# Where three kinds of small transfers are issued in a woven encoder step: head results, carried rows and cached keys

## The chip, the core and the metric

The kernel runs on one core of one Trainium2 chip. A time is the device time of one execution in microseconds (us), and the kernel's time is the median of several runs. The profile is of one execution; its trace lists every instruction with its start and length, and for idle time of an engine what ended it.

The engines are TensorE (PE: matmuls and transposes, its weight loads apart as PEld), VectorE (DVE), ScalarE (ACT), GpSimd (POOL) and SyncE (SP), which here does nothing but issue transfers. Each engine takes its instructions in program order.

## The reference

One step of an encoder layer for two groups of rows that share all weights: a prompt of 2048 rows and 8 samples of 16 rows (128 in all), width 1024, everything in 32-bit floats.

```
h     = RMSNorm(x) * (1 + scale1) + shift1
cols  = h @ w_in                      # columns belong to four mixers A, B, C, D with 4 heads each
A: gated delta rule    B: stick-breaking attention
C: softmax attention with a forget bias    D: softmax attention over 9 chunks of 64 rows, with a relative bias
mixed = [A | rms_norm(B) * merge_g[0] | rms_norm(C) * merge_g[1] | rms_norm(D) * merge_g[2]]   # per head
x     = x + gate1 * (mixed @ w_o)
h     = RMSNorm(x) * (1 + scale2) + shift2
a, b  = causal_conv3(h @ w_up)        # the samples start from state_ffn_conv, 2 rows for each
x     = x + gate2 * ((silu(a) * b) @ w_down)
```

A head has 64 columns, so `merge_g` is a row of 64 numbers for each head of B, C and D. The samples attend to cached keys and values too: 1024 rows for each sample in B and C, 512 in D.

## The kernel before

**The work and its stages.** Two kinds of streams are woven into one program. The dense stream first makes the projection in four parts of 512 rows, then four feed-forward blocks of 512 rows (the last also takes the 128 sample rows, and is called block 3 here). The mixer stream runs the delta rule and the attention of B, C and D for one part after another; such a stretch, one letter and one part, is called a pool here, since it has a tile pool of its own. There are 12 of them, with 4 heads each, so 48 heads. The samples' attention for B, C and D runs beside the parts. While a mixer waits for a chain through DVE, ACT and POOL, TensorE is to work on dense matmuls. The order of the instructions on each engine is set by `weave` and `merge`, which take turns between the streams, and then by the tile scheduler, which goes by a simulated timeline with priorities. So an edit that changes when something is due can move rows of the program far from it.

**Transfers.** Nearly all are issued from SP in program order, only some start-up loads from POOL. Eight semaphores (DMAHW0 to DMAHW7) are used in turn, so a transfer of SP waits until the one eight before it has landed. An instruction of SP that waits also holds all that is queued behind it.

**A head.** `head(h)` loads the head's queries `qT`, the forget bias (C) or the relative bias (D) as `add`; `start_k` and `start_v` load its keys `kT` and values `vhl`. `front` makes the scores (on TensorE `z<-kT,qT`) and weights, `back` the products with the values (`oT`). At the end of a head's last unit, `head_norm` (from L863) does this:

```
mg = A.sp.tile([P, 64], F32, name="hg", bufs=1)
nc.sync.dma_start(out=mg, in_=K.I["merge_g"][0, gi, h:h + 1].to_broadcast([P, 64]))
sq = A.sp.tile([P, nt, 64], F32, name="nsq", bufs=1)
...
nc.gpsimd.tensor_tensor(sq, sq, mg.unsqueeze(1).to_broadcast([P, nt, 64]), op=ALU.mult)
nc.sync.dma_start(out=dst, in_=sq)
```

POOL squares (L869), DVE sums (L871), a reciprocal root of several Newton steps follows between DVE and POOL (L203 to L217), DVE scales (L873), POOL multiplies by the gain (L874), and SP stores 128 KB to `mixed` (L875). `nsq` has one buffer, so the next head's squaring also waits until the store has landed. On POOL there also run the products of pool B's weights (L743), clears of parts of the tiles `wh` and `wl` (L834, L835) and the copies of feed-forward rows (L1890, L1915).

**Cached keys of the samples.** `keys` (from L1542) loads 512 rows of a sample's cached keys as one tile `ck` of 512 KB with one buffer (L1533), turns them with 8 transposes on TensorE (`ptr<-ident,ck`), and copies the result to `ckT` in two copies, taken in turn by DVE (L71) and ACT (L73). There are 40 such loads. The projected q and k of the new rows come first, in tiles of the same names (L1502).

**Feed-forward block 3.** Its start loads the weights `w_o` (in tiles `wu`, L1801), then `mixed` (in tiles `raw`, L1690), which TensorE turns (`d<-ident,raw`) before the product with `w_o`. For each chunk of 128 of the 5632 up-projected columns, in 44 calls of `up(fi)`, the carried rows of `state_ffn_conv` are loaded as a tile `stn` of 16 x 128 (8 KB, L1896, two buffers) and turned on TensorE (`ptr<-ident,stn`). The tiles `wd` (L1937) hold weights of the down-projection.

Of the kernel before, what the change touches and what calls it, by code (L numbers as in the profile page):

```python
# [5 lines left out]
F32 = mybir.dt.float32  # L6
# [9 lines left out]
P = 128  # L16
# [843 lines left out]
                nc.vector.tensor_scalar(oh[:, i - base, :], po[:, y * 64:y * 64 + 64], rls[i - 2 * jj], None, op0=ALU.mult)  # L860


def head_norm(K, A, gi, h, oh, nt, dst):  # L863

    nc = K.nc
    mg = A.sp.tile([P, 64], F32, name="hg", bufs=1)
    nc.sync.dma_start(out=mg, in_=K.I["merge_g"][0, gi, h:h + 1].to_broadcast([P, 64]))
    sq = A.sp.tile([P, nt, 64], F32, name="nsq", bufs=1)
    nc.gpsimd.tensor_tensor(sq, oh, oh, op=ALU.mult)  # L869
    ss = K.small.tile([P, nt], F32, name="nss")  # L870
    nc.vector.tensor_reduce(ss, sq, axis=AX.X, op=ALU.add)  # L871
    r = rsqrt(K, K.small, ss, nt, 1.0 / 64, EPS, "rsn")
    nc.vector.tensor_tensor(sq, oh, r.unsqueeze(2).to_broadcast([P, nt, 64]), op=ALU.mult)  # L873
    nc.gpsimd.tensor_tensor(sq, sq, mg.unsqueeze(1).to_broadcast([P, nt, 64]), op=ALU.mult)  # L874
    nc.sync.dma_start(out=dst, in_=sq)  # L875


def attn_prompt(K, g, part):


    nc = K.nc
    gi = "BCD".index(g)
# [3 lines left out]
    A = Ctx()  # L886
# [12 lines left out]
    def head(h):  # L899
        H = Ctx()  # L900
        H.h, H.kT, H.v = h, {}, {}
        H.qT = A.sp.tile([P, 2, 512], F32R, name="qT", bufs=2)
        nc.sync.dma_start(out=f(H.qT), in_=rows(K.qT[g][part], h))
        H.oh = A.sp.tile([P, 4, 64], F32, name="oh", bufs=2)
        if g == "C":
            fb = A.sp.tile([P, s1 * 512], F32, name="add", bufs=1)
            nc.sync.dma_start(out=fb.rearrange("p (t c) -> p t c", c=P),
                              in_=K.nF[0:16 * s1].rearrange("(t h) p -> h t p", h=4)[h:h + 1].to_broadcast([P, 4 * s1, P]))
            H.add = lambda a, b, c1: fb[:, a:b]
        if g == "D":  # L910
            bias = A.sp.tile([P, 640], F32, name="add", bufs=2)
            nc.sync.dma_start(out=bias, in_=K.toep(h))
            nc.gpsimd.memset(bias[0:64, 576:640], NEG)
            nc.gpsimd.memset(bias[64:128, 0:64], NEG)
            H.add = lambda a, b, c1: bias[:, a + 640 - c1:b + 640 - c1]
        return H
# [43 lines left out]
    def back(u):  # L960
        H, jj = u.H, u.jj
        if u.first:
            u.st.V = Values(K, A, jj, lo, u.st.wts, H.v, *((2 * jj, 0) if g == "B" else (lo(2 * jj), 2 * jj)))
        for a in u.groups:
            u.st.V.group(a)
            yield
        if u.last:
            u.st.V.finish(None if g == "B" else [w.rl for w in u.st.wts], H.oh, 4 * part)
            if jj == j0 + 1:
                yield  # L970
                r, c = 4 * part * P, (1 + gi) * 256 + H.h * 64
                head_norm(K, A, gi, H.h, H.oh, 4, K.mixed[r:r + 512, c:c + 64].rearrange("(t p) d -> p t d", p=P))

    units = []
    for h in range(4):
        hs = Ctx()
        hs.h = h
        for jj in (j0, j0 + 1):
            st = Ctx()
            for s in range(jj // 2, -1, -1) if g == "B" else [None]:  # L980
                u = Ctx()
# [26 lines left out]
    with K.tc.tile_pool(name=f"a{g}{part}", bufs=2, side="right", reuse_waits="tile") as A.sp:  # L1008
        yield from start_k(units[0])
        for n, u in enumerate(units):  # L1010
            u.H = u.hs.H
            parts = [(front(u), u.nf)]
            if n:
                b = units[n - 1]
# [474 lines left out]
def samples_steps(K, A, g):  # L1489
    nc, I, sp, psum = K.nc, K.I, A.sp, A.psum  # L1490
    gi = "BCD".index(g)
    name = {"B": "sb", "C": "fox", "D": "band"}[g]
    ck, cv = I[f"cache_{name}_k"], I[f"cache_{name}_v"]
# [4 lines left out]
        segs = segs[::-1]  # L1498
    x0 = []
    for n, src in (("k", K.qs[g]), ("v", K.ks[g])):  # L1500
        t = sp.tile([P, 4 if n == "k" else 2, 256], F32, name="c" + n, bufs=1 if n == "k" else 2)[:, 0]
        nc.sync.dma_start(out=t, in_=src)  # L1502
        x0.append(t)
    qn, kn = x0
# [8 lines left out]
    if g == "D":  # L1513
        bias = sp.tile([P, 640], F32, name="sbias", bufs=1)
        for h in range(8):
            r = slice(h * 16, h * 16 + 16)
# [3 lines left out]
    pt = psum()  # L1520
# [3 lines left out]
    for o in range(2):  # L1524
        r = slice(o * 64, o * 64 + 64)
# [3 lines left out]

    def load(b, s):  # L1530

        t = sp.tile([P, 4, 256], F32, name="ck", bufs=1)
        nc.sync.dma_start(out=t, in_=ck[0, b, s * 512:(s + 1) * 512].rearrange("(t p) h d -> p t (h d)", p=P))  # L1533
        return t

    def load_v(b, kt):

# [4 lines left out]
    def keys(L, b, s):  # L1542

        L.kT[s] = []
        for u in range(2):
            k = load(b + u, s)
            kT = sp.tile([P, 2, 512], F32, name="ckT", bufs=2)
            L.kT[s].append(kT)
            for x in range(2):
                pt = psum()  # L1550
                for j in range(4):
                    K.pe.transpose(pt[:, j * P:(j + 1) * P], k[:, j, x * P:x * P + P], K.ident)
                A.ev.copy(kT[:, x], pt)
                yield

    def weights(L, b):
# [80 lines left out]
NF = 22  # L1637
# [133 lines left out]
def feed_block(K, B, sa, sp, nxt, pool, copies):  # L1771


    nc, I, O = K.nc, K.I, K.O
    T, tiles, GM, ahead, acc, p = B.T, B.tiles, B.GM, B.ahead, B.acc, B.p
    smp = NP in tiles
# [62 lines left out]
    n = len(tiles)  # L1839
    pt = K.dps()  # L1840
# [32 lines left out]
    def carry():  # L1873
# [8 lines left out]
            nc.sync.dma_start(out=O["ffn_conv_s"][:, cc], in_=eo[2:18])  # L1882
        late.clear()

    def up(fi):

        cw = K.fcw[:, fi]
# [4 lines left out]
        if smp:  # L1892
            us = u[:, 2 + Tp:2 + Tp + NB * 18].rearrange("p (b s) -> p b s", s=18)
            parts.append((lambda i: us[:, :, i:i + 16], s16(yv[:, Tp:T])))
            stn = sp.tile([16, P], F32, name="stn", bufs=2)
            nc.sync.dma_start(out=stn, in_=I["state_ffn_conv"][0, :, :, fi * P:(fi + 1) * P].rearrange("b r c -> (b r) c"))  # L1896

        def evict(ps, c0, c1):
            m = min(c1, Tp)
# [262 lines left out]
```

## Time and profile before

| | |
|---|---|
| median of 3 runs | 3899.07 us (3897.04 to 3899.76) |
| the profiled execution's own time | 3892.44 us |
| its span in the trace | 3890.7 us |
| mean granted TensorE clock | 0.967 |
| TensorE busy | 3628.3 us, 93% of the span |
| VectorE, ScalarE, GpSimd busy | 2437.3, 1537.0, 1406.7 us |
| moved by transfers | 830.36 MB, 213 GB/s in the mean |

The span lies 1.7 us below the execution's own time. The profiled execution is 6.6 us faster than the median of the runs.

In the rows of the trace that follow, a row of the timeline has the start, the length, the engine and line, the operation, the tile written and the tiles read, how many rows were merged, and in brackets how long the engine had been idle and what ended that. `SPq` is the issue of a transfer on SP: its length is that of the issuing, not of the transfer. A row of the list of waits says who waited, for whom, and then the total in us, how often, and the longest. A group of one line has the shortest, median and longest duration in ns.

### The profile page before, as it was taken

To read this page: it belongs to the slowest core of one execution; us is meant where nothing else is said; L and a number is where in the kernel's file an instruction comes from. 1 tells how busy PE (TensorE), PEld (TensorE's weight loads), DVE (VectorE), ACT (ScalarE), POOL (GpSimd) and SP (SyncE) were. 2 spreads that over 40 slices of the span, in tenths; PEclk is the share of its full clock that TensorE was granted. 3 is DMA by queue.
4 is the path that set the end of the run, shared out by engine and by line. 5 is a ranking of instruction groups with operands and counts; after the bars stand their busy time and mean duration, and the time that the engine had idled before them with its cause. 6 is when DMAs were issued, how large, how long until landed. Compare 5 with 4: busy or idle time off the path is not lost.

```text
span 3890.7 us, 66224 instructions
## 1 busy us (share of the span) xinstructions
PE 3628.3 (93%) x22763; PEld 3147.3 (81%) x22763; DVE 2437.3 (63%) x5592; ACT 1537.0 (40%) x3352; POOL 1406.7 (36%) x3487
## 2 busy tenths in 40 slices
PE   6998899989988999999999999989999987899999
PEld 4887889989986667767877888668887876899999
DVE  5668556465676876877595656755875665344344
ACT  3455223343454533543463533413553443232221
POOL 4456244363333444434571112323652122122121
PEclk7999999999998999999999999999999998899999
DMA  7887868877668798987536555665445545444442
GB/s 225 290 279 245 300 199 299 295 256 246 218 227 255 254 307 274 306 293 270 200 120 213 171 201 169 226 209 178 158 148 182 177 123 206 141 149 137 153 143 93
DMA packets 529077, 830.36 MB, mean 213 GB/s; under 512 B 112651, under 2 KB 351260, under 8 KB 528477
## 3 DMA queue, kind: packets, MB, share of 16 engines
q1 hardware_dynamic: 527269, 825.16, 64.2%
q8 instruction: 181, 2.97, 0.3%
q0 software_dynamic: 1472, 0.97, 0.1%
q14 instruction: 155, 1.26, 0.1%
HBM read 611.81 MB, written 224.16 MB: 215 GB/s over the span
## 4 chain that ended last, share of the span: by engine, by line
PE 62%; DMA 11%; DVE 9%; POOL 4%; issue 3%; ACT 2%; SPq 1%; POOLq 0%; DVEq 0%; ACTq 0%
PE d L89 44%; PE z L89 5%; PE oT L89 5%; PE ptr L92 4%; PE ptr L89 2%; PE d L92 1%; DVE pr L741 1%; DMA w<-win 1%; DMA add<-nF 1%; DVE gy L1184 1%; DVE cv L1913 1%; DMA wraw<-in_ada_w_dram 1%; DMA raw<-in_x_prompt_dram 1%; PE z L92 1%; DVE acc L1823 1%
## 5 line engine op out<-in xcount | busy, mean ns | idle before, releaser
L89 PE MATMUL d<-hh,wu 128*128 128x512 f32 (+1 forms) x3520 | 1013.9, 364 | 2.8 <-DMA wu<-keptw_up 1.6
L89 PEld LDWEIGHTS d<-hh,wu 128*128 128x128 f32 x3520 | 635.2, 190 | 94.6 <-issue 8.6
L89 PE MATMUL d<-w,hh 128*128 128x256 f32 (+2 forms) x3536 | 679.3, 288 | 30.3 <-DMA w<-win 9.7
L89 PE MATMUL d<-hl,wu 128*128 128x512 f32 (+1 forms) x1760 | 638.8, 363 | 0.8 <-DVE hl L1863 0.7
L89 PEld LDWEIGHTS d<-w,hh 128*128 128x128 f32 x3536 | 557.6, 191 | 48.6 <-DVE w L459 11.8
L89 PE MATMUL d<-gh,wd 128*128 128x512 f32 (+1 forms) x1760 | 529.8, 369 | 10.3 <-DVE acc L1823 8.1
L89 PE MATMUL d<-w,hl 128*128 128x256 f32 (+2 forms) x1768 | 502.3, 286 | 0.2 <-DVE hl L408 0.2
L1913 DVE SCALAR_TENSOR_TENSOR cv<-u,fcw,cv 128x512 f32<-128x512 f32 (+1 forms) x440 | 300.1, 705 | 174.2 <-ACT cv L1911 170.9
L1823 DVE SCALAR_TENSOR_TENSOR acc<-d,mod,acc 128x512 f32<-128x512 f32 (+2 forms) x432 | 280.8, 656 | 188.4 <-PE d L89 187.1
L89 PEld LDWEIGHTS d<-hl,wu 128*128 128x128 f32 x1760 | 334.0, 190 | 43.9 <-DVE hl L1863 3.0
L89 PEld LDWEIGHTS d<-gh,wd 128*128 128x128 f32 x1760 | 319.1, 189 | 60.3 <-DVE acc L1823 13.6
L89 PEld LDWEIGHTS d<-w,hl 128*128 128x128 f32 x1768 | 336.3, 191 | 4.8 <-issue 3.3
L89 PE MATMUL d<-gl,wd 128*128 128x512 f32 (+1 forms) x880 | 319.4, 363 | 0.0
L89 PE MATMUL z<-kT,qT 128*128 128x512 f32 (+3 forms) x864 | 255.8, 385 | 34.7 <-DMA kT<-kTD 13.8
L840 ACT CAST wh<-ptr 128x512 fp32r<-128x512 f32 (+1 forms) x372 | 197.4, 552 | 226.8 <-PE ptr L92 133.6
L841 DVE TENSOR_TENSOR wl<-ptr,wh 128x512 fp32r<-128x512 f32 (+1 forms) x372 | 232.3, 639 | 79.5 <-ACT wh L840 69.1
L1900 ACT COPY u<-d 128x512 f32<-128x512 f32 (+1 forms) x220 | 109.9, 500 | 396.5 <-PE d L89 391.0
L92 PE MATMUL ptr<-ident,w 128*128 128x128 f32 x1448 | 225.1, 277 | 18.9 <-POOL w L743 8.2
L741 DVE TENSOR_TENSOR_SCAN pr<-sn,pr,zeros 128x512 f32<-128x512 f32 (+3 forms) x172 | 217.8, 1275 | 24.3 <-ACT sn L733 18.8
L1915 POOL COPY hal<-u 128x2 f32<-128x2 f32 x176 | 44.5, 254 | 519.7 <-ACT u L1900 516.2
L743 POOL TENSOR_TENSOR w<-w,pr 128x512 f32<-128x512 f32 (+3 forms) x168 | 190.8, 1138 | 112.1 <-DVE pr L741 60.2
L790 ACT ACTIVATE w<-w,nm 128x512 f32<-128x512 f32 (+3 forms) x284 | 174.1, 615 | 120.5 <-DVE nm L783 98.1
(610 smaller groups left out, 7116.5 us busy)
## 6 DMA issues: line engine op xcount, KB each, us to landing
wu<-keptw_up SPq DMA_DIRECT2D x264, 512.0 KB
w<-win SPq DMA_DIRECT2D x132, 512.0 KB
wd<-keptw_down SPq DMA_DIRECT2D x132, 512.0 KB
keptw_up<-wu SPq DMA_DIRECT2D x88, 512.0 KB
wu<-keptw_o SPq DMA_DIRECT2D x48, 512.0 KB
win<-w SPq DMA_DIRECT2D x44, 512.0 KB
raw<-in_w_up_dram SPq DMA_DIRECT2D x88, 256.0 KB
keptw_down<-wd SPq DMA_DIRECT2D x44, 512.0 KB
```

The costliest lines, as they stand in the source:

```text
L89: return self.note(self.nc.tensor.matmul(out, lhsT, rhs, **k))
L92: return self.note(self.nc.tensor.transpose(*a, **k))
L741: nc.vector.tensor_tensor_scan(out=pr[:, 0:m][:, ::-1], data0=sn[:, :m][:, ::-1], data1=K.zeros[:r, :m], initial=carry, op0=ALU.mult, op1= ...
L743: nc.gpsimd.tensor_tensor(w[:, :m], w[:, :m], pr[:, 1:m + 1], op=ALU.mult)
L790: self.K.nc.scalar.activation(w, w, AF.Exp, bias=self.nm, accum_out=self.l[:, s:s + 1])
L840: nc.scalar.copy(wh[:, c0:c1], pt[:, c0:c1])
L841: nc.vector.tensor_tensor(wl[:, c0:c1], pt[:, c0:c1], f(wh[:, c0:c1]), op=ALU.subtract)
L1184: nc.vector.scalar_tensor_tensor(yc, tap(c, i), self.cw[:, c, i:i + 1], yc, op0=ALU.mult, op1=ALU.add)
L1823: nc.vector.scalar_tensor_tensor(acc[k][:, c0:m], ps[:, :m - c0], gate[:, k, 0:1], acc[k][:, c0:m], op0=ALU.mult, op1=ALU.add)
L1900: nc.scalar.copy(u[:, 2 + c0:2 + m], ps[:, :m - c0])
L1913: nc.vector.scalar_tensor_tensor(o, tap(i), cw[:, i:i + 1], o, op0=ALU.mult, op1=ALU.add)
L1915: nc.gpsimd.tensor_copy(K.hal[:, fi], tail)
```

## The change

It has three parts.

- In the attention over the prompt, the gain tile `hg` is loaded in `head()` together with the head's queries, with two buffers, no longer in `head_norm`. The store to `mixed` is issued by POOL, right behind the multiply, no longer by SP. `nsq` keeps its one buffer.
- A tile `ck` of the samples holds 256 rows (256 KB) in place of 512, with two buffers. There are twice as many loads, with as many transposes and copies as before; a copy now takes both column halves of two row blocks and writes them to two places of `ckT`.
- The carried rows `stn` of block 3 are loaded three chunks ahead: three loads at the start of the block, then one in each `up`, into four buffers in place of two.

```
-def head_norm(K, A, gi, h, oh, nt, dst):
+def head_norm(K, A, mg, oh, nt, dst):
...
-    mg = A.sp.tile([P, 64], F32, name="hg", bufs=1)
-    nc.sync.dma_start(out=mg, in_=K.I["merge_g"][0, gi, h:h + 1].to_broadcast([P, 64]))
     sq = A.sp.tile([P, nt, 64], F32, name="nsq", bufs=1)
...
-    nc.sync.dma_start(out=dst, in_=sq)
+    nc.gpsimd.dma_start(out=dst, in_=sq)
...
         H.oh = A.sp.tile([P, 4, 64], F32, name="oh", bufs=2)
+        H.mg = A.sp.tile([P, 64], F32, name="hg", bufs=2)
+        nc.sync.dma_start(out=H.mg, in_=K.I["merge_g"][0, gi, h:h + 1].to_broadcast([P, 64]))
...
-        t = sp.tile([P, 4 if n == "k" else 2, 256], F32, name="c" + n, bufs=1 if n == "k" else 2)[:, 0]
+        t = sp.tile([P, 2, 256], F32, name="c" + n, bufs=2)[:, 0]
...
     def load(b, s):
 
-        t = sp.tile([P, 4, 256], F32, name="ck", bufs=1)
-        nc.sync.dma_start(out=t, in_=ck[0, b, s * 512:(s + 1) * 512].rearrange("(t p) h d -> p t (h d)", p=P))
-        return t
+        ts = [sp.tile([P, 2, 256], F32, name="ck", bufs=2) for _ in range(2)]
+        for n, t in enumerate(ts):
+            c = s * 512 + n * 256
+            nc.sync.dma_start(out=t, in_=ck[0, b, c:c + 256].rearrange("(t p) h d -> p t (h d)", p=P))
+        return ts
...
-            k = load(b + u, s)
             kT = sp.tile([P, 2, 512], F32, name="ckT", bufs=2)
             L.kT[s].append(kT)
-            for x in range(2):
+            for n, k in enumerate(load(b + u, s)):
                 pt = psum()
-                for j in range(4):
-                    K.pe.transpose(pt[:, j * P:(j + 1) * P], k[:, j, x * P:x * P + P], K.ident)
-                A.ev.copy(kT[:, x], pt)
+                for x in range(2):
+                    for j in range(2):
+                        c = (2 * x + j) * P
+                        K.pe.transpose(pt[:, c:c + P], k[:, j, x * P:x * P + P], K.ident)
+                A.ev.copy(kT[:, :, n * 256:n * 256 + 256], pt.rearrange("p (x n) -> p x n", x=2))
                 yield
...
+    state, ahead_of = [], [c for j in range(NF) for c in (j, NF + j)] if smp else []
+
+    def state_load():
+
+        if ahead_of:
+            fi = ahead_of.pop(0)
+            state.append(sp.tile([16, P], F32, name="stn", bufs=4))
+            nc.sync.dma_start(out=state[-1], in_=I["state_ffn_conv"][0, :, :, fi * P:(fi + 1) * P].rearrange("b r c -> (b r) c"))
+
+    for _ in range(3):
+        state_load()
...
-            stn = sp.tile([16, P], F32, name="stn", bufs=2)
-            nc.sync.dma_start(out=stn, in_=I["state_ffn_conv"][0, :, :, fi * P:(fi + 1) * P].rearrange("b r c -> (b r) c"))
+            stn = state.pop(0)
+            state_load()
```

SP has 2661 transfers before and 2653 now (48 stores fewer, 40 key loads more). Below stand SP's rows at three places, each with what the row waits for: DMAHW is the landing of an earlier transfer of SP, DMASW of one of POOL, and Pool, PE, DVE and Activation are engines.

The first place is the end of pool C and the start of pool D, both of part 3, before:

```order
L1801 DMA wu_38524<-keptw_up_89 128x1024 [waits DMAHW3_49,PE_49]
L875 DMA mixed_80<-nsq_38004 128x4x64 [waits DMAHW0_49,Pool_49]
L903 DMA qT_38033<-qTD_116 128x1024 [waits DMAHW1_49,DVE_49]
L912 DMA add_38036<-skew_3924 128x640
L998 DMA kT_38040<-kTD_114 128x512 [waits PE_49,Activation_49]
L998 DMA kT_38042<-kTD_114 128x512 [waits DMAHW4_49]
```

The same place now (line numbers are a few higher in the changed kernel):

```order
L1805 DMA wu_38606<-keptw_up_89 128x1024 [waits DMAHW4_49,DMAHW0_49,PE_49]
L902 DMA qT_38113<-qTD_116 128x1024 [waits DVE_49]
L905 DMA hg_38116<-in_merge_g_dram 128x64
L913 DMA add_38118<-skew_3924 128x640
L999 DMA kT_38122<-kTD_114 128x512 [waits PE_49,Activation_49]
L999 DMA kT_38124<-kTD_114 128x512 [waits DMAHW1_49]
```

The store of pool C's last head, which waits for POOL, stood ahead of pool D's first loads; it is on POOL's queue now, and pool D's first hg takes a place there that waits for no engine.

The second place is inside that pool D, where its first two heads end, before (`out_0` are stores of block 2's results):

```order
L875 DMA mixed_80<-nsq_38425 128x4x64 [waits Pool_49]
L867 DMA hg_38765<-in_merge_g_dram 128x64 [waits DMAHW6_49]
L1735 DMA out_0_dram<-raw_38736 128x512 [waits DMAHW7_49,Activation_49]
L1735 DMA out_0_dram<-raw_38744 128x512 [waits DMAHW0_49,DVE_49]
L1735 DMA out_0_dram<-raw_38801 128x512 [waits DMAHW1_49,Activation_49]
L1735 DMA out_0_dram<-raw_38809 128x512 [waits DMAHW2_49,DVE_49]
L1005 DMA vhl_39092<-vhlD_115 128x512 [waits DMAHW3_49,PE_49]
L875 DMA mixed_80<-nsq_38767 128x4x64 [waits DMAHW4_49,Pool_49]
L867 DMA hg_39063<-in_merge_g_dram 128x64 [waits DMAHW6_49,DMAHW5_49]
```

The same place now:

```order
L905 DMA hg_38678<-in_merge_g_dram 128x64 [waits Pool_49]
L1739 DMA out_0_dram<-raw_38820 128x512 [waits DMAHW3_49,Activation_49]
L1739 DMA out_0_dram<-raw_38828 128x512 [waits DMAHW4_49,DVE_49]
L1739 DMA out_0_dram<-raw_38883 128x512 [waits DMAHW5_49,Activation_49]
L1739 DMA out_0_dram<-raw_38891 128x512 [waits DMAHW6_49,DVE_49]
L1006 DMA vhl_39174<-vhlD_115 128x512 [waits DMAHW7_49,PE_49]
L905 DMA hg_39033<-in_merge_g_dram 128x64 [waits DMAHW0_49,Pool_49]
```

The stores of heads 0 and 1 are gone from here, and the gains of heads 2 and 3 stand in their places; each waits for POOL, because the buffer that it takes is free only when the multiply of the head two before is done. In the whole program 24 of the 48 loads of hg wait for POOL in this way, those of heads 2 and 3 of each pool.

The third place is the start of block 3, before (the rows ahead of these are the eight `wu` loads of w_o, two `stn` and one `hg`):

```order
L875 DMA mixed_80<-nsq_39065 128x4x64 [waits DMAHW5_49]
L1937 DMA wd_40799<-keptw_down_90 128x1024 [waits DMAHW6_49]
L1937 DMA wd_40801<-keptw_down_90 128x1024 [waits DMAHW7_49]
L1937 DMA wd_40803<-keptw_down_90 128x1024 [waits DMAHW0_49]
L1937 DMA wd_40905<-keptw_down_90 128x1024 [waits DMAHW1_49]
L1937 DMA wd_40907<-keptw_down_90 128x1024 [waits DMAHW2_49]
L1937 DMA wd_40909<-keptw_down_90 128x1024 [waits DMAHW3_49]
L1896 DMA stn_40292<-in_state_ffn_conv_dram 16x128 [waits DMAHW4_49,PE_49]
L1896 DMA stn_40375<-in_state_ffn_conv_dram 16x128 [waits DMAHW5_49,PE_49]
L875 DMA mixed_80<-nsq_39232 128x4x64 [waits DMAHW6_49,Pool_49]
L1896 DMA stn_40462<-in_state_ffn_conv_dram 16x128 [waits DMAHW7_49,DMAHW4_49,PE_49]
L1690 DMA raw_39263<-mixed_80 128x512 [waits DMAHW0_49]
```

The same place now; the rows ahead of these are the eight `wu` and the first three `stn`:

```order
L1896 DMA stn_40214<-in_state_ffn_conv_dram 16x128 [waits DMAHW0_49]
L1953 DMA wd_40885<-keptw_down_90 128x1024 [waits DMAHW1_49]
L1953 DMA wd_40887<-keptw_down_90 128x1024 [waits DMAHW2_49]
L1953 DMA wd_40889<-keptw_down_90 128x1024 [waits DMAHW3_49]
L1953 DMA wd_40991<-keptw_down_90 128x1024 [waits DMAHW4_49]
L1953 DMA wd_40993<-keptw_down_90 128x1024 [waits DMAHW5_49]
L1953 DMA wd_40995<-keptw_down_90 128x1024 [waits DMAHW6_49]
L1896 DMA stn_40291<-in_state_ffn_conv_dram 16x128 [waits DMAHW7_49,PE_49]
L1896 DMA stn_40378<-in_state_ffn_conv_dram 16x128 [waits DMAHW0_49,PE_49]
L1896 DMA stn_40461<-in_state_ffn_conv_dram 16x128 [waits DMAHW1_49,PE_49]
L1896 DMA stn_40548<-in_state_ffn_conv_dram 16x128 [waits DMAHW2_49,PE_49]
L1694 DMA raw_39343<-mixed_80 128x512 [waits DMASW6_49,DMASW5_49,DMAHW3_49,DMASW4_49,DMASW3_49]
```

Four `stn` stand ahead of the `wd` loads in place of two, and both stores have left SP. The first loads of `mixed` now wait for landings of pool B's stores on POOL; the sixth, the first that reads columns of C and D, waits for all of POOL's. On TensorE four transposes of `stn` stand ahead of those of `raw`, before and now.

More of the change, by code (lines that the diff above doesn't have):

```diff
@@ L971, in back @@
                 r, c = 4 * part * P, (1 + gi) * 256 + H.h * 64
-                head_norm(K, A, gi, H.h, H.oh, 4, K.mixed[r:r + 512, c:c + 64].rearrange("(t p) d -> p t d", p=P))
+                head_norm(K, A, H.mg, H.oh, 4, K.mixed[r:r + 512, c:c + 64].rearrange("(t p) d -> p t d", p=P))
     units = []
```

## Prediction

> **What bounds the kernel now.** I read the page first, then the list of who waited for whom, then the two windows of the timeline in which TensorE stands longest.
>
> ```profile
> span 3890.7 us, 66224 instructions
> PE 3628.3 (93%) x22763; PEld 3147.3 (81%) x22763; DVE 2437.3 (63%) x5592; ACT 1537.0 (40%) x3352; POOL 1406.7 (36%) x3487
> PE 62%; DMA 11%; DVE 9%; POOL 4%; issue 3%; ACT 2%; SPq 1%; POOLq 0%; DVEq 0%; ACTq 0%
> ```
>
> The second line gives the busy time of each engine, the third the chain that ended last. TensorE is the bound: it idles for 3890.7 − 3628.3 = 262.4 us of the span, and no edit here takes a matmul or a transpose away. What can be won is part of those 262.4 us. What matters is therefore not how long an engine or queue waits, but whether TensorE stands still behind it. The list of waits names the candidates (in total, times, longest, all in us):
>
> ```profile
> PE ptr L92 <- DMA stn<-in_state_ffn_conv_dram: 18.3, 2, 9.6
> PE z L89 <- DMA kT<-kTD: 13.8, 1, 13.8
> PE ptr L92 <- DMA ck<-in_cache_sb_k_dram: 7.1, 2, 3.6
> PE ptr L92 <- DMA ck<-in_cache_fox_k_dram: 1.3, 2, 1.0
> SPq L875 <- POOL nsq L874: 85.1, 24, 9.1
> SPq L875 <- POOL wl L835: 23.3, 8, 14.7
> SPq L875 <- POOL wh L834: 9.9, 2, 9.5
> ```
>
> The last three rows are SP's own queue. The result store (L875) stood for 85.1 + 23.3 + 9.9 = 118.3 us until POOL had multiplied by the gain. Nearly all transfers are issued from SP in program order, so each wait holds everything behind it. Yet only the first four rows are waits of TensorE, 40.5 us in all: the 118.3 us are not the gain.
>
> **The store of head results, on SP before, on POOL after.** By the order of the program, half of the 118.3 us isn't removed at all. The gain tile hg now has two buffers, and its load for heads 2 and 3 of each pool waits on POOL until the multiply of heads 0 and 1 has read the buffer; it stands on SP about where the store of those heads stood. So 24 of the 48 SP waits go and 24 stay under another name; by count, 59 us go. Where the removed ones cost TensorE something, the timeline must say. It does at one place, where head 3 of pool C, part 3, ends and pool D begins. SP's rows there:
>
> ```profile
> 3208.84 0.37 SPq L875 DMA_DIRECT2D mixed<-nsq  x1
> 3209.30 0.46 SPq L903 DMA_DIRECT2D qT<-qTD  x1
> 3209.80 0.44 SPq L912 DMA_DIRECT2D add<-skew  x1
> 3210.34 0.86 SPq L998 DMA_DIRECT2D kT<-kTD  x2
> ```
>
> and POOL's and TensorE's, where the bracket is the idle time before a row and what ended it:
>
> ```profile
> 3208.09 0.72 POOL L874 TENSOR_TENSOR nsq<-nsq,hg 128x256 f32<-128x256 f32 x1 [0.54 <-DVE nsq L873]
> 3200.73 0.55 PE L89 MATMUL oT<-j,os 128*128 128x64 f32 x4
> 3215.05 1.83 PE L89 MATMUL z<-kT,qT 128*128 128x512 f32 x4 [13.76 <-DMA kT<-kTD]
> 3216.68 0.63 PE L89 MATMUL d<-gh,wd 128*128 128x512 f32 x1
> 3220.09 0.73 PE L89 MATMUL d<-gh,wd 128*128 128x512 f32 x2
> 3220.66 0.40 PE L89 MATMUL d<-gl,wd 128*128 128x512 f32 x1
> 3220.89 0.40 PE L89 MATMUL d<-gh,wd 128*128 128x512 f32 x1
> ```
>
> TensorE's last matmuls of head 3 (3200.73) start head 3's norm chain; POOL's multiply ends it at 3208.81, SP's store goes at 3208.84, and only then pool D's q, bias and keys. The keys land 4.7 us after their issue (3210.34 to 3215.05). In the new order no wait on head 3 stands ahead of them: hg for pool D's first heads waits on no engine, and what SP waits for there, the last feed-forward weights and the transposes of pool C, is done before TensorE reaches 3200.73. If SP issues the keys by 3196, they land by 3200.7 and the next z matmuls run on. Nothing else of pool D is late behind them: its queries and its bias go out ahead of the keys. Term: −13.8 us.
>
> TensorE is also slow after the gap. From 3215.05 to 3220.09 it starts 4 + 8 matmuls of 512 columns, 0.42 us apart; at 3220.66 to 3220.89 the step is 0.23. Twelve times 0.19 is 2.3 us, which goes with the gap if the gap causes it. Term: −2.3.
>
> The other 23 removed waits I cost at nothing, since no row of TensorE's waits stands behind them; TensorE has feed-forward matmuls meanwhile. If that cover is gone, it shows as new gaps at z<-kT.
>
> **What the store costs on POOL.** No store of this shape is on POOL now. SP's own row, POOL's 16 loads of 9 pieces of 1 KB, and its one load of 192 pieces of 480 bytes (smask, 64 partitions by 3):
>
> ```profile
> L875 SPq DMA_DIRECT2D mixed<-nsq x48: 359/371/1224, 192.3 to 3305.2; - x48
> L293 POOL DMA_DIRECT2D abia<-in_ada_b_dram x16: 520/587/611, 72.8 to 494.0; - x16
> L247 POOL DMA_DIRECT2D smask<-in_smask_dram x1: 732/732/732, 5.9 to 5.9; - x1
> DMA to landing us min/median/max: 2.7/5.1/6.3
> ```
>
> The fourth row belongs to L293. The store writes 4 pieces of 256 bytes for each of 128 rows, 512 pieces. If POOL's price is one per transfer it is 0.6 us; if it goes with the pieces, 0.732 × 512 / 192 = 1.95 us. A line through the two rows, (732 − 587) / 183 = 0.8 ns for a piece, gives 0.59 + 0.40 = 1.0 us, and I take that: 48 us on an engine busy for 1406.7 of 3890.7. Cover: behind the store stand POOL's products of the weights, and TensorE waits for those 8.2 us in the whole run (quoted with the rivals). I cost it at 0; its ends are 0 and 48 × 1.95 = 94 us, of which the slow rival takes a part. On SP, 48 × 0.37 = 18 us of issuing go and 40 extra key loads come; neither is on TensorE's path.
>
> The Trainium skill ("SBUF — State Buffer", section "SBUF: two separate sides") speaks against this part: a transfer issued from POOL has its descriptors written by GpSimd cores, which VectorE's copies can lock out of the shared port. The rows of L293 show no such stretch: 520 to 611 ns, all 16 within a sixth, on a kernel where VectorE is busy 63% of the time; but they have 9 pieces each, so for 512 the rule stays open, and would bring the slow rival.
>
> **The carried rows, three chunks ahead.** At the start of feed-forward block 3:
>
> ```profile
> 3283.64 3.96 SPq L1801 DMA_DIRECT2D wu<-keptw_o  x8
> 3287.64 1.50 SPq L1896 DMA_DIRECT2D stn<-in_state_ffn_conv_dram  x2
> 3291.83 0.39 SPq L875 DMA_DIRECT2D mixed<-nsq  x1
> 3293.11 5.22 SPq L1937 DMA_DIRECT2D wd<-keptw_down  x6
> 3298.42 0.84 SPq L1896 DMA_DIRECT2D stn<-in_state_ffn_conv_dram  x2
> 3305.20 0.39 SPq L875 DMA_DIRECT2D mixed<-nsq  x1
> 3307.26 4.22 SPq L1690 DMA_DIRECT2D raw<-mixed  x8
> ```
>
> ```profile
> 3297.35 0.55 PE L92 MATMUL ptr<-ident,stn 16*128 16x16 f32 x2 [9.58 <-DMA stn<-in_state_ffn_conv_dram]
> 3306.61 0.43 PE L92 MATMUL ptr<-ident,stn 16*128 16x16 f32 x2 [8.71 <-DMA stn<-in_state_ffn_conv_dram]
> 3310.01 2.03 PE L92 MATMUL d<-ident,raw 128*128 128x128 f32 x8 [2.98 <-DMA raw<-mixed]
> 3313.20 2.18 PE L92 MATMUL d<-ident,raw 128*128 128x128 f32 x9 [1.16 <-DMA raw<-mixed]
> 3298.88 0.61 POOL L869 TENSOR_TENSOR nsq<-oh 128x256 f32<-128x256 f32 x1 [8.78 <-DMA mixed<-nsq]
> ```
>
> TensorE idles 9.58 + 8.71 + 2.98 + 1.16 = 22.4 us. In the new order all four stn tiles that TensorE transposes first stand right behind the same eight 512 KB loads of w_o. The first gap therefore stays (they land at 3297.4 as before), the second goes. But what is late next stands close: raw<-mixed. Its loads are issued behind the six wd loads (3 MB, which before had the stn behind them land at 3306.6), and the second half of the columns waits for head 3's store. That store can't go before head 2's has landed, since nsq has one buffer: from POOL it would be issued at about 3290.1 (3289.38 + 0.72), land 2.7 to 6.3 us later by L293's row, and head 3's chain from L869 to its store takes 6.3 us (3298.88 to 3305.20); its own landing adds 2.7 to 6.3 more: 3302 to 3310. With wd issued some 3 us sooner, raw's first tiles should reach TensorE at 3304 to 3308, against 3310.0. Term: −4; ends +3 (head 3's store lands late behind the weights) and −12 (all but the first gap goes).
>
> **Cached keys in halves.** A half of 256 KB lands sooner and two can be under way. TensorE's waits for ck are 7.1 + 1.3 = 8.4 us in four places. In that stretch DMA moves 258 GB/s (first row: PE, PEld, DVE, ACT and POOL busy, clock, DMA share, GB/s), so half a tile is 1.0 us:
>
> ```profile
> 180.00:1420.00 1240.00, 1148.79 (x8364) 1031.47 (x8363) 811.83 (x2067) 520.02 (x1138) 550.45 (x1548) 0.97 0.78 258
> L71 DVE COPY ckT<-ptr x45: 670/681/693, 1192.7 to 2538.0; 128x512 f32<-128x512 f32 x45
> ```
>
> Transposes and copies keep count and size (two 0.68 us copies for each tile, now strided). Term: −3, between −8.4 and +3 (a strided copy as much as 0.04 us dearer, 80 times).
>
> **Sum.** −13.8 − 2.3 − 4 − 3 = −23.1 us. The profiled execution took 3892.44 us, so 3869.3 by its scale. The median of the three runs, 3899.07, lies 6.6 above it, so I expect 3876 as median. The instruction order moves in many other places (on TensorE over four rows in ten stand elsewhere), which I put at ±8, an estimate: 3% of the idle 262.4.
>
> **The rivals.** *No change.* The wait is swapped, not taken away: half of the SP waits stay as hg waits, and what the reordering brings back as TensorE idle elsewhere eats 15 to 23 us. Against it: the 13.76 us gap has one cause, which is gone. For it: 59 us of SP waiting remain, any of which may now stand ahead of something urgent. Time 3891 to 3902. The Trainium skill ("DMA: Bandwidth & Descriptors", "Issuing engines are not separate DMA queues") holds that another issuing engine only saves issue time, 48 × 0.37 us here, off the path, which would also be no change; the trace disagrees where the time is the queue's wait, not its issue (3208.84).
>
> *Slower: POOL's store is dear and lies on pool B's chain.* There POOL multiplies the weights that TensorE transposes:
>
> ```profile
> L92 PE MATMUL ptr<-ident,w 128*128 128x128 f32 x1448 | 225.1, 277 | 18.9 <-POOL w L743 8.2 <-ACT w L790 4.4 <-DVE wl L841 2.8
> ```
>
> Pool B has 16 stores; at 1.95 us each, wholly on the path, they cost 31 us: 3876 + 31 = 3907. That is the point from which it ends slower. If pools C and D, whose POOL clears parts of the weights' tiles, pay a third of theirs as well, it is 3907 + 32 × 0.65 = 3928. The 8.2 us speak against it: there is slack.
>
> *More gain.* Only the first stn gap stays (−12 in place of −4) and all ck waits go (−8.4 in place of −3): 3876 − 13 = 3863.
>
> **Chances.** Forecast (3866 to 3888) 0.60, more gain (3855 to 3866) 0.13, no change (3891 to 3902) 0.18, slower (3907 to 3928) 0.09. A measurement tells about 0.2% from no change, 7.8 us: faster is below 3891.3, slower above 3906.9. So faster 0.73, same 0.18, slower 0.09. A range from 3856 to 3897 leaves out the slower case, the upper half of no change and a rest below, together 2 in 10.
>
> **What the profile after would show.** Right: no gap above 2 us at pool D's first z<-kT in part 3; one stn gap of about 9.6 ahead of the last w_o product, not two, and 2 to 6 us less from it to raw<-mixed; hg loads waiting on POOL for some 59 us; POOL's store at 0.6 to 1.2 us; ck waits under 6 us. Wrong: a kT<-kTD wait of several us anywhere; POOL's store above 1.9 us or its landing above 10, with TensorE waiting for L743 far over 8.2; new gaps before 1000 us worth more than 8.

## The result, and the profile after

The changed kernel takes 3917.09 us in the median (3912.55 to 3925.72, 4 runs) against 3898.30 for the kernel before (4 runs): the ratio is 1.005, with a 95% interval of 1.0034 to 1.0066. It is slower by 18.8 us, where 22 us of a gain were forecast. Its profiled execution took 3913.41 us; the span and the busy times are these:

```profile
span 3911.6 us, 66285 instructions
PE 3649.6 (93%) x22763; PEld 3162.4 (81%) x22763; DVE 2444.6 (62%) x5592; ACT 1533.1 (39%) x3350; POOL 1436.5 (37%) x3535
```

TensorE idles for 3911.6 − 3649.6 = 262.0 us, as long as before (262.4). The 20.9 us between the two spans are therefore TensorE's busy time, 3649.6 against 3628.3 us for the same 22763 matmuls. Part of that is the execution's own pace: the trace of e3 below has 3645.1 us of it, with TensorE's rows as before up to 3458 us. How much of the 21.3 us is the new order's stays open.

The longest waits of the changed kernel that bear on the change, those of TensorE first, then those of SP for POOL:

```profile
PE d L92 <- DMA raw<-mixed: 12.3, 6, 7.8
PE ptr L92 <- DMA stn<-in_state_ffn_conv_dram: 11.2, 1, 11.2
PE z L89 <- DMA kT<-kTD: 10.0, 2, 9.6
PE ptr L92 <- DMA ck<-in_cache_sb_k_dram: 4.2, 2, 3.2
PE ptr L92 <- DMA ck<-in_cache_fox_k_dram: 2.8, 2, 2.2
PE ptr L92 <- POOL w L743: 2.4, 4, 0.9
SPq L905 <- POOL nsq L873: 72.9, 16, 11.4
SPq L905 <- POOL wl L835: 6.8, 4, 5.6
SPq L905 <- POOL pr L736: 6.1, 1, 6.1
```

A wait for kT<-kTD of 9.6 us is there, of the kind that the prediction had named as a sign of being wrong. It is not the one that was to go. At the end of pool C of part 3, SP issues pool D's loads without waiting for head 3, and what is late next is the bias (timeline of the changed kernel, SP, then TensorE, VectorE and POOL):

```profile
3227.95 0.42 SPq L902 DMA_DIRECT2D qT<-qTD  x1
3230.74 0.80 SPq L999 DMA_DIRECT2D kT<-kTD  x2
...
3235.18 1.09 PE L89 MATMUL z<-kT,qT 128*128 128x512 f32 x4 [0.37 <-DMA kT<-kTD]
3244.90 0.69 PE L89 MATMUL z<-kT,qT 128*128 128x128 f32 x2 [5.86 <-DVE mx L773]
...
3244.15 0.69 DVE L773 CUSTOM_DVE_ANT_0 w<-z,add 128x512 f32<-128x512 f32 x1 [2.58 <-POOL add L915]
...
3242.67 0.79 POOL L874 DMA_DIRECT2D mixed<-nsq  x1 [0.29 <-POOL nsq L873]
3243.74 0.17 POOL L914 MEMSET add<- 64x64 f32 x1
```

The keys come 0.37 us late in place of 13.76. Then VectorE waits for the two fills of pool D's bias (L914, L915), and these stand on POOL behind the whole norm chain of pool C's last head and its store. Of the 13.76 us of idle, 5.86 come back here.

The new 9.59 us are 890 us earlier, where pool D of part 2 begins. First the changed kernel, then the kernel before:

```profile
2337.98 6.44 SPq L1953 DMA_DIRECT2D wd<-keptw_down  x4
2344.52 0.38 SPq L902 DMA_DIRECT2D qT<-qTD  x1
2345.95 0.87 SPq L999 DMA_DIRECT2D kT<-kTD  x2
...
2353.67 1.83 PE L89 MATMUL z<-kT,qT 128*128 128x512 f32 x4 [9.59 <-DMA kT<-kTD]
```

```profile
2287.44 1.00 SPq L1937 DMA_DIRECT2D wd<-keptw_down  x2
2290.06 0.37 SPq L875 DMA_DIRECT2D mixed<-nsq  x1
2290.86 0.32 SPq L1801 DMA_DIRECT2D wu<-keptw_up  x1
2291.27 0.38 SPq L903 DMA_DIRECT2D qT<-qTD  x1
```

After, pool D's first loads stand behind four wd loads that wait for TensorE to release buffers (10.0 us in SP's list of waits for that stretch). The kernel before has its first scores of this pool at 2301.32 us, without a wait. Pool D's loads go out 53 us later than before; some 14 of these can be the execution's own pace, since in e3, with the order of before, they go at 2305.61. That lag begins at pool B of part 2, again first after, then before:

```profile
1906.51 26.49 SPq L1805 DMA_DIRECT2D wu<-keptw_o  x9
1938.44 0.43 SPq L902 DMA_DIRECT2D qT<-qTB  x1
```

```profile
1889.70 0.32 SPq L1801 DMA_DIRECT2D wu<-keptw_o  x1
1891.51 0.43 SPq L903 DMA_DIRECT2D qT<-qTB  x1
1898.62 1.69 SPq L1801 DMA_DIRECT2D wu<-keptw_o  x3
```

Before, part 2's first queries go out after the seventh of the 16 loads of a block's w_o; after, they stand behind all 16, of which the last nine take 26.5 us, since they wait for TensorE to release buffers.

### The profile page after: what moved, and what is told of

The parts are those of the page before. It is cut to its first block, busy times and chain, and to the rows that moved or that the text cites. A ratio compares the mean times of both kernels' runs of the same rounds, so it can differ in the third digit from the quotient of the medians.

```text
span 3911.6 us, 66285 instructions
## 1 busy us (share of the span) xinstructions
PE 3649.6 (93%) x22763; PEld 3162.4 (81%) x22763; DVE 2444.6 (62%) x5592; ACT 1533.1 (39%) x3350; POOL 1436.5 (37%) x3535
## 4 chain that ended last, share of the span: by engine, by line
PE 56%; DMA 8%; DVE 7%; POOL 3%; issue 2%; ACT 2%; SPq 1%; DVEq 0%; POOLq 0%; ACTq 0%
PE d L89 40%; PE z L89 5%; PE oT L89 4%; PE ptr L92 4%; PE ptr L89 1%; DMA add<-nF 1%; PE d L92 1%; DVE pr L741 1%; DMA raw<-in_w_up_dram 1%; DVE cv L1929 1%; DVE wl L841 1%; PE z L92 1%; DMA raw<-in_x_prompt_dram 1%; DMA out_dram<-raw 1%; DMA raw<-in_w_down_dram 1%
## 5 line engine op out<-in xcount | busy, mean ns | idle before, releaser
L89 PEld LDWEIGHTS d<-hh,wu 128*128 128x128 f32 x3520 | 634.2, 189 | 92.2 <-issue 8.8
L89 PE MATMUL z<-kT,qT 128*128 128x512 f32 (+3 forms) x864 | 256.9, 386 | 35.8 <-DVE mx L773 13.2
L743 POOL TENSOR_TENSOR w<-w,pr 128x512 f32<-128x512 f32 (+3 forms) x168 | 186.6, 1113 | 118.5 <-DVE pr L741 56.8
L773 DVE CUSTOM_DVE_ANT_0 w<-z,add 128x512 f32<-128x512 f32 (+3 forms) x272 | 146.7, 555 | 101.8 <-PE z L89 51.9
```

The costliest lines, as they stand in the source:

```text
L89: return self.note(self.nc.tensor.matmul(out, lhsT, rhs, **k))
L743: nc.gpsimd.tensor_tensor(w[:, :m], w[:, :m], pr[:, 1:m + 1], op=ALU.mult)
L773: nc.vector.tensor_tensor_reduce(out=w[:, :m], in0=ps[:, :m], in1=self.addend(c0, c1), op0=ALU.add, op1=ALU.max, scale=1.0, scalar=-3.0e38 ...
```

## The experiments

Each kernel is compared with the kernel before, measured beside it. Differences are of medians. The ratio stands on record with its 95% interval and is not the quotient of the two medians, so the two can lie some us apart (e10: 12.7 us by the medians, 9.8 by the ratio). Executions of the kernel before lay between 3884.84 and 3912.95 us, so only medians of many runs tell a few us, and single traces are read for places more than for sums.

**The parts one by one.** e1: `head_norm` as changed (gains early, store on POOL), the rest as before.

> Only the first part: gains loaded with the head's inputs, results stored from POOL; key tiles and carried rows as before. Theory A (the store part costs): the loss of 19 us comes with the store, through POOL's queue (0.79 us for each of 48) or the gains' waits, so this kernel alone is 15 to 25 us slower than before. Theory B (scatter): the store part does what was forecast at the end of pool C of part 3 (13.8 us of idle gone, 9 us gained there) and costs nothing by itself; every edit changes the order in which the scheduler puts the rows, and with it where TensorE pauses and how many of its matmuls fall into stretches of half clock; then this kernel lies anywhere within 15 us of before, and the three parts alone do not add up to 19. In both the gap at pool D's first scores of part 3 is under 7 us.

Measured 3913.48 against 3897.51, 1.0037 (1.0024 to 1.005): 16.0 us over, in the range of theory A and just outside that of theory B. At pool D of part 3 the gap is 5.89 us, as both had it.

e2: only `ck` in halves.

> Only the cached keys in halves. Theory A: 0 to 4 us faster than before, since TensorE's waits for these tiles were 8.4 us and nothing else is touched. Theory B: the rows move far from the samples' attention too, and the time can change by 5 to 15 us either way, with more or fewer matmuls in half clock.

Measured 3918.14 against 3897.51, 1.0052 (1.0035 to 1.0069): slower by 20.6 us. That is outside both forecasts. Its trace has the gap at pool D of part 2, though no store and no gain tile was touched:

```profile
2347.55 1.83 PE L89 MATMUL z<-kT,qT 128*128 128x512 f32 x4 [8.84 <-DMA kT<-kTD]
```

e3: only the carried rows three chunks ahead.

> Only the carried rows three chunks ahead. Theory A: 2 to 8 us faster, by the second wait for stn at the start of block 3 (8.7 us), and the trace up to 3200 us as before. Theory B: the same there, since nothing after 3300 us can be reordered far, but if rows before 3200 us move, 5 to 15 us either way.

Measured 3895.66 against 3897.51, 0.9992 (0.998 to 1.0004). TensorE's second wait for stn is gone, but raw<-mixed is late in its stead:

```profile
3311.88 0.43 PE L92 MATMUL ptr<-ident,stn 16*128 16x16 f32 x2 [9.69 <-DMA stn<-in_state_ffn_conv_dram]
...
3323.97 1.97 PE L92 MATMUL d<-ident,raw 128*128 128x128 f32 x8 [10.95 <-DMA raw<-mixed]
```

e4: the changed kernel with the store back on SP.

```
-    nc.gpsimd.dma_start(out=dst, in_=sq)
+    nc.sync.dma_start(out=dst, in_=sq)
```

> The changed kernel with the store put back on SP (gains early, key halves, carried rows ahead stay). Theory A: if POOL's issuing of the store is what costs, this kernel is 10 to 20 us faster than the changed one, though the gap of 13.8 us at the end of pool C of part 3 is back. Theory B: no such step; 14 us of idle come back at pool C's end and the rest is another draw, so between 10 us faster and 20 us slower than the changed kernel.

Measured 3899.19 against 3897.51, 1.0004 (0.999 to 1.0017). It is some 18 us faster than the changed kernel, as theory A had it and more than theory B allowed, so taken alone it speaks for A; e7, e8 and e13 below decide against it. It holds the key halves, which alone were 20.6 us over before, and lies within the noise of before. The parts do not add: 16.0 + 20.6 − 1.9 is 34.7, the changed kernel measured 18.8.

**Gains, queue and POOL's time.** e5: gains early, the store on SP.

> Only the gains loaded early, with two buffers; the store stays on SP, keys and carried rows as before. On SP, pool D of part 2 has its first loads behind the same later group of four wd loads as in the changed kernel and in the one with key halves alone. Theory B (order): a gap of 7 to 10 us at pool D's first scores near 2350 us, the gap of 13 to 15 us at the end of pool C of part 3 is back, and the time is 8 to 20 us over before. Theory A (POOL's store costs): no store on POOL, so within 4 us of before.

Measured 3902.20 against 3896.80, 1.0012 (1.0001 to 1.0023): 5.4 us, between the two forecasts. The place was right:

```profile
2340.58 1.83 PE L89 MATMUL z<-kT,qT 128*128 128x512 f32 x4 [10.87 <-DMA kT<-kTD]
```

e6: as e1 with `nc.scalar.dma_start` for the store.

> Gains early, the store issued by ScalarE's queue in place of POOL's. SP is as free as with POOL. Theory A: POOL keeps its work of before, so the loss of 16 us of the store on POOL goes, and with the gap at pool C's end gone the time is 5 to 15 us under before. Theory B: another order, so another draw: from 10 us under to 15 us over before; no gap of 9 us near 2350 us, since pool D's loads stand ahead of the wd group there.

Measured 3905.81 against 3896.80, 1.0016 (1.0007 to 1.0026): POOL is free of the store, and the kernel is 9 us slower by the medians, 6 by the ratio.

e7: only the store on POOL, gains as before.

> The store on POOL, the gains still loaded at the head's end by SP with one buffer, keys and carried rows as before. Theory A: the loss of 16 us is there, 12 to 20 us over before. Theory B: another draw, and no gap near 2350 us; the gap at the end of pool C of part 3 is under 7 us. If the early gains' waits on POOL cost, this kernel is faster than the one with early gains and the store on POOL.

Measured 3901.96, 1.0013 (1.0003 to 1.0023): 5 us over, not 12 to 20.

e8: the kernel before, with two more copies on POOL for each head. In the trace they take 44.3 us in all, 0.9 us a head, in place of the 1.2 us that was expected.

```
     nc.sync.dma_start(out=dst, in_=sq)
+    for _ in range(2):
+        nc.gpsimd.tensor_copy(oh, oh)
```

> The kernel before, and behind each of the 48 stores POOL copies the head's result onto itself twice, which changes no value: some 1.2 us more of POOL's time for each head, about as much as a store on POOL takes there, with the store still on SP. Theory A: POOL's time costs, so 12 to 20 us over before. Theory B: POOL's time is hidden; the order changes again, so within 12 us of before either way.

Measured 3901.61, 1.0009 (0.9999 to 1.0019). With e7, theory A falls in these orders: neither POOL's time nor the store on POOL costs 16 us.

**The order kept, and the order alone changed.** e9: one store of the 48 on POOL.

```
-    nc.sync.dma_start(out=dst, in_=sq)
+    q.dma_start(out=dst, in_=sq)   # q: nc.gpsimd if (g, part, H.h) == ("C", 3, 3) else nc.sync
```

> The kernel before, with one store of the 48 on POOL: that of the last head of pool C, part 3. TensorE's rows stand exactly as before. Theory B (the local gain is real, the loss comes from the reordering): the gap of 13.8 us at pool D's first scores falls to 4 to 7 us, where VectorE's maximum is late next, and the time is 6 to 13 us under before. Theory A (the store on POOL costs, a little for each): the same, since one store can't cost much. If the time does not fall, the gap's gain is lost again behind it, at the start of block 3.

Measured 3891.40 against 3901.02, 0.9976 (0.9963 to 0.9989): faster by 9.6 us. The gap:

```profile
3216.79 0.69 PE L89 MATMUL z<-kT,qT 128*128 128x128 f32 x2 [6.52 <-DVE mx L773]
```

e10: the same with `part == 3` as the condition (12 stores), and the carried rows ahead.

> The kernel before, with the 12 stores of part 3 on POOL and the carried rows three chunks ahead; gains loaded as before, keys as before. TensorE's order is as before up to block 3. Theory B: 8 to 18 us under before: the gap at pool D's first scores falls to 4 to 7 us and block 3 starts some 3 us sooner. Theory A: a quarter of the 16 us of the 48 stores is paid, so 4 us less of a gain.

Measured 3888.36 against 3901.02, 0.9975 (0.9964 to 0.9986).

e11 and e12: the kernel before with another order of the same work, by the table of paces: `"B0": 0.91` in place of 0.9, and `PHI = 1.01` in place of 1.0.

> The kernel before with one number of the weave's table changed, the pace of pool B of part 0 from 0.90 to 0.91. The work is the same; most of TensorE's rows move, as many as in the changed kernel. Theory B: the order alone moves the time, and before is a good draw, so 0 to 20 us over before. Theory A: no work is added and no wait, so within 4 us of before.

> The kernel before with all paces of the weave 1% higher, the same work in another order. Theory B: a second draw, 0 to 20 us over before. Theory A: within 4 us of before.

Measured 3894.99, 0.998 (0.9968 to 0.9992), and 3900.82, 0.9999 (0.9989 to 1.0009), against 3901.02. Neither of these two orders is slower than that of before, so nothing says that the kernel before is a lucky draw; that part of theory B was not borne out. e11 is 6 us faster, outside both forecasts.

**The changed kernel and the key halves in other orders.** e13 is the changed kernel with `PHI = 1.01`, e14 the changed kernel with `"B0": 0.91`.

> The changed kernel with all paces of the weave 1% higher (which left the kernel before where it was). In this order pool D's first loads of part 2 no longer stand behind the later group of four wd loads. Theory B (the loss is the order's luck): no gap of 9 us near 2350 us, and the time falls by 8 to 25 us against the changed kernel, to before or under it. Theory C (taking the stores off SP costs in any order, some 20 to 25 us net of the 10 us gained at the end of pool C of part 3): 10 to 20 us over before again.

> The changed kernel with the pace of pool B of part 0 at 0.91 (which made the kernel before 6 to 8 us faster). Here the group of four wd loads still stands ahead of pool D's first loads of part 2, so the gap of 8 to 11 us near 2350 us is there under every theory. Theory B: another draw, from 15 us under to 5 us over the changed kernel. Theory C: 8 to 18 us over before.

Measured against 3897.28: e13 3887.46, 0.9974 (0.9962 to 0.9985), faster than before by 9.8 us with every edit in it; e14 3915.73, 1.0051 (1.0035 to 1.0066). In e13 the first loads of pool B and pool D of part 2 are early again:

```profile
1876.97 0.42 SPq L902 DMA_DIRECT2D qT<-qTB  x1
...
2292.05 0.38 SPq L902 DMA_DIRECT2D qT<-qTD  x1
```

e15: the key halves alone with `PHI = 1.01`; e16: e10 with `"B0": 0.91`.

> Only the key halves, with all paces 1% higher. Pool D's first loads of part 2 stand ahead of the later wd group again. Theory B: the 20 us that the key halves alone cost were the order's; the gap near 2350 us is gone and the time is within 8 us of before. If key halves themselves cost, it is 15 to 20 us over before as without the pace.

> The stores of part 3 on POOL and the carried rows ahead, with the pace of pool B of part 0 at 0.91. If the two gains (10 to 12 us and 6 to 8 us against before) stand in different places, they add: 14 to 20 us under before. Theory B allows less, since the pace moves the rows at the end of pool C of part 3 as well: not under 5 us of a gain.

Measured 3892.86, 0.9988 (0.9976 to 0.9999) for e15: the 20.6 us of the key halves are gone. For e16, 3892.01, 0.9985 (0.9973 to 0.9997), 5.3 us under before: the two gains did not add.

**The late start alone.** e17: the kernel before, with the queries and keys of pool B's first head of part 2 held on SP.

```
+                if w == "w_up" and c == 0 and q == 0:
+                    K.first_up = ld
...
+        if (g, part, u.hs.h) == ("B", 2, 0):
+            with K.tc.issue_after(K.first_up.ins):
+                H = u.hs.H = head(u.hs.h)
```

> The kernel before with one thing forced: the loads of queries, keys of the first head of pool B of part 2 are held on SP until the block's first w_up load has been issued, as the order of the changed kernel, of the key halves alone and of the changed kernel with pool B's pace at 0.91 has it. The work is the same, no store moves, the keys are whole; TensorE's rows are as before until that place. If this late start of part 2's pools is what cost those kernels their time: pool B's first query load goes near 1925 to 1940 us in place of 1890 to 1905, the gap of 8 to 11 us at pool D's first scores near 2350 us appears, and the time is 10 to 20 us over before. If it is not the cause, within 5 us of before.

Measured 3911.03 against 3899.05, 1.0031 (1.0019 to 1.0044): 12 us slower, with the same work. SP's rows, and TensorE's gap at pool D:

```profile
1896.41 21.88 SPq L1809 DMA_DIRECT2D wu<-keptw_o  x9
...
1921.06 0.42 SPq L903 DMA_DIRECT2D qT<-qTB  x1
...
2321.57 6.47 SPq L1947 DMA_DIRECT2D wd<-keptw_down  x4
2329.64 0.37 SPq L875 DMA_DIRECT2D mixed<-nsq  x1
2330.10 0.45 SPq L903 DMA_DIRECT2D qT<-qTD  x1
...
2335.73 1.83 PE L89 MATMUL z<-kT,qT 128*128 128x512 f32 x4 [8.04 <-DMA kT<-kTD]
```

Only these loads of pool B were held; pool D's place behind four wd loads followed from it. TensorE's rows in e17 stand as in the kernel before up to 1904 us and again from 2656 us on. For the 3750 matmuls between these two points the kernel before takes 738.2 us, of which TensorE idles 38.1; e3 and e9, which have the order of before there, take 745.2 and 741.9 us and idle 40.0 and 40.1; e17 takes 751.9 us and idles 54.1. So the loss shows as 14 to 16 us more of idle time in this stretch, the 8.04 us at pool D among them. Some 3000 of these matmuls stand elsewhere than before; what the late loads cost by themselves and what this reordering behind them costs is not told apart.

Five of the 19 kernels measured have pool B's first queries of part 2 behind all 16 w_o loads: the changed one, e2, e5, e14 and e17. All five are slower than before, by 5.4 to 20.6 us. The other 14 lie between 12.7 us under before and 16.0 over (e1), so the late start is not the only cost that an order can bring.

e18: e1 with `PHI = 1.01`.

> Gains early and the store on POOL, as in the first experiment (16 us over before), with all paces of the weave 1% higher. If the store part itself costs, 10 to 16 us over before again. If those 16 us were the order's, the time is between 12 us under and 5 us over before.

Measured 3901.18 against 3899.05, 1.0 (0.9989 to 1.0011): the 16 us of e1 are gone in this order.

## Why the prediction was wrong

The step that failed is the last of the sum: "The instruction order moves in many other places (on TensorE over four rows in ten stand elsewhere), which I put at ±8, an estimate: 3% of the idle 262.4." That number came from no row. The order after was in hand, and read only at the places where the edits are. At the start of part 2's pools, which no edit touches, it put the first loads behind a whole block's w_o loads. The terms before it come to about −11.5 us by e9 (−9.6) and e3 (−1.9), with nothing for the key halves (e15), in place of −23.1; from there to +18.8 the order brought some 30 us, where ±8 was allowed. The forecast was also made of idle time, with 2.3 us for slow matmuls. In the traces of before and after the idle time is the same, so what was gained and what was newly lost cancel there, and the difference is busy time.

e17 shows what forcing the late start into the kernel before costs: 12 us. With it the changed kernel measured 18.8 us over before, in the order of e14 18.5, and without it, in e13, 9.8 under. If the late start costs the changed kernel as much as it cost e17, that is 12 of the 28.6 us between its two orders; this is argued, since effects do not add here. The traces of the changed kernel and of e13 lie 32.0 us apart in their spans, 18.8 of them idle and 13.2 busy time. Two rows of the lists of waits are about as large as the idle part: TensorE's scores wait 10.0 us for kT<-kTD in the changed kernel and not at all in e13, and its transposes wait 11.2 us for stn in the one and 0.2 in the other. So the start of block 3 went another way with the pace as well. For the busy part I can name no place. That e1 lost 16 us without the late start, and which rows of its order cost them, stays open; only that they go with the order is shown (e18). Why the late start comes with some edits was not tried; e5 has it too and lost only 5.4 us.

Point by point:

- **The 13.8 us at pool D of part 3.** Right in kind: the wait for head 3's store is gone. "Nothing else of pool D is late behind them: its queries and its bias go out ahead of the keys" was wrong: the bias also needs POOL, where its fills stand behind head 3's chain, and a store on POOL adds its 0.79 us to that. Of 13.8 + 2.3 us, e9 gained 9.6.
- **The hg waits.** Forecast 59 us on SP, measured 92.2 us in 24 waits: the three rows above, and 4.8 and 1.6 us in two smaller ones. Whether a load that TensorE waits for is late because of one of them, these lists do not tell; at pool D of part 2 and of part 3 it is not so.
- **POOL's price.** Forecast 1.0 us for a store, between 0.6 and 1.95:

```profile
L874 POOL DMA_DIRECT2D mixed<-nsq x48: 788/791/849, 193.8 to 3330.9; - x48
DMA to landing us min/median/max: 2.4/3.7/7.9
```

  Measured: 0.79 us for a store, all 48 within a tenth of each other, with VectorE busy 62% of the time, and a landing after 3.7 us in the median; TensorE's waits for L743 fell from 8.2 to 2.4 us. The rule of the Trainium skill ("SBUF — State Buffer", "SBUF: two separate sides") that VectorE can starve a transfer issued from POOL does not show in these issue times of 0.788 to 0.849 us. Whether it has a part in the landings of 2.4 to 7.9 us is open, as no trace here tells which of VectorE's instructions are of the kind that the page names. The slow rival's mechanism did not come about (e8, e13); the result had its sign by another.
- **The carried rows.** −4 was forecast, e3 measured −1.9 with an interval that holds zero. The second stn wait went as forecast, and raw<-mixed, "late next", took nearly all of it: its loads still stand behind the six wd loads (timeline after, SP and TensorE).

```profile
3314.31 4.56 SPq L1896 DMA_DIRECT2D stn<-in_state_ffn_conv_dram  x4
3319.84 5.70 SPq L1953 DMA_DIRECT2D wd<-keptw_down  x6
3328.05 8.93 SPq L1694 DMA_DIRECT2D raw<-mixed  x10
...
3324.40 0.99 PE L92 MATMUL ptr<-ident,stn 16*128 16x16 f32 x4 [11.21 <-DMA stn<-in_state_ffn_conv_dram]
3333.17 4.17 PE L92 MATMUL d<-ident,raw 128*128 128x128 f32 x20 [7.78 <-DMA raw<-mixed]
```

- **The key halves.** TensorE's waits for ck fell from 8.4 to 4.2 + 2.8 = 7.0 us, so −1.4 for −3. The +3 of the range, for a strided copy dearer by 0.04 us, was in no row and did not come: the copies to ckT take 0.681 us on VectorE and 0.585 on ScalarE before, 0.680 and 0.586 after. In e15's order the key halves cost nothing.
- **The rivals.** "No change" had named the right kind of loss, something urgent put behind a wait, though it looked for it behind the waits for hg, where the runs show weight loads, and priced it at 15 to 23 us of the gain. The order weighs more than that: the same edits in two orders, the changed kernel's and e13's, lie 28.6 us apart, from +18.8 to −9.8. My size was bounded by the idle time that was there, not by what a late pool can add.

Of the kernels run, e10, e13 (every edit, another pace) and e9 are the fastest: by 12.7, 9.8 and 9.6 us against before. e11, e16 and e15 are 4.4 to 6.0 us faster.

## What to carry to other kernels

Where a scheduler sets the order, an edit has two effects: the one it was made for, at its place, and a new order everywhere else. Read in the new order where each stream's first loads stand, and behind which waits, also in places that no edit touches. Test an edit in two or three orders of the same work, or confine it to the place where it gains, before the edit itself is blamed or praised. Here the same edits measured +18.8 and −9.8 us.

## What the runs showed of the hardware

The profiled e3 has the program of before up to 3283 us, yet its span is 3903.9 us against 3890.7, and its granted clock 0.962 against 0.967. In the stretch from 250 to 450 us, long ahead of the first difference, the rows of before and then of e3 are these (the stretch, its length, busy time of PE, PEld, DVE, ACT and POOL, the granted clock, DMA share, GB/s):

```profile
250.00:450.00 200.00, 168.03 (x1250) 153.23 (x1250) 159.54 (x407) 95.46 (x199) 111.25 (x298) 0.96 0.82 271
```

```profile
250.00:450.00 200.00, 175.61 (x1232) 161.04 (x1233) 156.57 (x406) 94.52 (x198) 109.12 (x299) 0.90 0.81 268
```

The granted clock is 0.96 in one and 0.90 in the other, with the same instructions in the same order; TensorE needs 7.6 us more for fewer of them. So the spans of two single traces of this kernel can lie 13 us apart by the execution alone, with medians that are 2 us apart, and the profile of before, 6 us under the median, was a quick one.
